# Token mixer of one decoder layer: the triangular inverse's recurrence spread over 128 partitions, its transpose made by products, the keys' chain given priority

## The chip, the cores and the metric

The kernel runs on one NeuronCore of a Trainium2 chip. The time is the device time of one execution in microseconds, on the slowest (here the only) core. The trace is that of one profiled execution of the program.

## The reference

One layer of an autoregressive decoder over 512 tokens of width 2048, all in float32. RMSNorm is followed by one input projection, whose columns feed three mixers in parallel: differential attention (4 heads), sliding-window attention (8 query heads, 2 key heads, window 128) and an RWKV-7 time mix (16 heads of 64). Their outputs are joined, projected, and added to the input; then come RMSNorm, a SwiGLU feed-forward of 5632 hidden units, a second addition, and a last RMSNorm. The change touches only the RWKV-7 part, whose definition is a scan over the tokens:

```python
kk = hs(k * k_k.astype(f32))
kk = kk / jnp.maximum(jnp.sqrt(jnp.sum(kk * kk, axis=-1, keepdims=True)), 1e-12)
k = k * (1.0 + (a - 1.0) * k_a.astype(f32))
...
y = wkv7_scan(r4, hs(decay), k4, v4, -kk, kk * a4)
...
def step(S, inp):
    r_t, w_t, k_t, v_t, a_t, b_t = inp
    sa = jnp.einsum('bhvk,bhk->bhv', S, a_t)
    S = S * w_t[:, :, None, :] + sa[..., None] * b_t[:, :, None, :] + v_t[..., None] * k_t[:, :, None, :]
    return S, jnp.einsum('bhvk,bhk->bhv', S, r_t)
```

## The kernel before, in words

**Dense work.** A projection item is 16 blocks of 128 input rows by 128 output columns against 512 tokens. Each float32 product is made of three products of a rounded format (high by high, high by low, low by high), so an item is 48 matmuls of 128 x 512, all through `mm`, line 130. `weights` (lines 203 to 208) loads half an item's weights by one DMA on the SP queue, casts the high part on ACT (line 207) and subtracts for the low part on DVE (line 208); the weights of the next item are asked for before the current one runs. The items run in this order: gates, then for each of eight pairs of RWKV heads k, r and v, then the attention heads, the output projection, and the feed-forward.

**Side work.** Everything of the mixers that is not a projection is written as Python generators in eight lanes. After each dense matmul `pump` lets every lane whose due time has come go one step. The due times come from `now`, a running estimate of the PE's time, and from `charge`, an estimate of when DVE and ACT will be done; `yield n` asks for n us of that estimate. The order of the PE's instructions is that order and is kept. On ACT, DVE, POOL and the DMA queues the compiler's scheduler puts the instructions in order by a priority, which is their place in the program unless a block raises it: `urgent` puts the state loop's copies at the program's start. When a projection is done, its `go` may have to wait for an older step (`need`): the k of a pair waits for the k of the pair before to be used up, the v for that pair's prep to end. Then only lanes run.

**A pair of RWKV heads.** Tokens are cut into 8 chunks of 64. For each pair:
- `rates` makes the decays; it begins when `prep` of the pair before has ended.
- `prep` normalises the keys (product `kn`, lines 509 to 512), makes `ar` (line 518, two buffers), `bk` (lines 526 and 531), turns `bk` on the PE in two halves (`bt`, line 540) into `bkn` once the state loop of the pair two before is done, makes the products `gr` (line 566) and masks them into `L`, `zl` and `gr` (line 574), and stores the four 32 x 32 diagonal blocks of each chunk of `L` to DRAM (`li`, line 585).
- `inverse` (lines 613 to 640) loads them as 32 matrices (2 heads, 2 blocks, 8 chunks), one whole matrix to a partition, and inverts the unit triangular matrices by a recurrence of 30 steps, two DVE instructions each (lines 629 and 630). It stores the result (`xi`) and, from a copy turned by ACT (line 633), its transpose (`xj`).
- `join` (lines 642 to 673) loads the inverted blocks back into `L` and the transposes of the first block of each head into `xn`, and makes the block off the diagonal by two sets of 16 products of 32 x 32 (`pt` and `po`).
- `chain` is the state loop over the 8 chunks, with products `z`, `u`, `S` and `y`; it begins when `post` of the pair before has read `y`. Its `y` products are the last readers of `ar`.
- `post` normalises and spills the result.

Of the kernel before, what the change touches and what calls it, by code (L numbers as in the profile page):

```python
# [8 lines left out]
F32 = mybir.dt.float32  # L9
F32R = mybir.dt.float32r  # L10
AF = mybir.ActivationFunctionType
ALU = mybir.AluOpType
AX = mybir.AxisListType

P = 128
# [4 lines left out]
C = 64  # L20
NCH = T // C
# [67 lines left out]
class Kernel:  # L89
    def __init__(self, tc, ins, out, dbg=None, stop=None):  # L90
        self.tc = tc
        self.nc = tc.nc
        self.i = ins
        self.out = out
        self.dbg = dbg or {}
        self.stop = stop
        self.lanes = [[], [], [], [], [], [], [], []]
        self.order = [self.lanes[j] for j in (2, 7, 6, 5, 0, 1, 3, 4)]
        self.done = set()
        self.flags = set()  # L100
        self.now = 0.0
        self.due = {}
        self.free = {"DVE": 0.0, "Activation": 0.0}
        self.last = 0.0
        self.slack = 0.3

    def col(self, name, j=0, n=P):
        c = COL[name] + j
        return self.cols[:n, c:c + 1]
# [383 lines left out]
    def prep(self, hp):  # L493
        nc, rp = self.nc, self.rp
        q = self.in_flight[hp]
        while "k" not in q or f"rates{hp}" not in self.done:
            yield
        W, V, a = q["W"], q["V"], q["a"]

        k = q["k"]  # L500
        rn = rp.tile([P, T], F32, tag="rn", name=f"rn{hp}")
        kk_g = self.col("k_k", hp)
        nc.scalar.activation(rn, k, AF.Square, scale=kk_g)
        yield
        ps = self.pm.tile([P, T], F32, tag="m", name=f"kn{hp}")
        self.mm(ps, self.cst("onesbd", P), rn, start=True, stop=True)
        kk = rp.tile([P, T], F32, tag="kk", name=f"kk{hp}")

        nc.scalar.activation(kk, ps, AF.Relu, bias=self.cst("knmin", 1))
        nc.scalar.activation(kk, kk, AF.Ln, bias=self.cst("kneps", 1))  # L510
        nc.scalar.activation(kk, kk, AF.Exp, scale=-0.5)
        nc.vector.scalar_tensor_tensor(out=kk, in0=k, scalar=kk_g, in1=kk, op0=ALU.mult, op1=ALU.mult)

        def c3(x):
            return x.rearrange("p (n c) -> p n c", c=C)

        ar = rp.tile([P, NCH, 2, C], F32, tag="ar", name=f"ar{hp}", bufs=2)
        nc.vector.scalar_tensor_tensor(out=ar[:, :, 0, :], in0=c3(kk), scalar=-1.0, in1=W[:, :, 0:64],
                                       op0=ALU.mult, op1=ALU.mult)
        bk = rp.tile([P, NCH, 2, C], F32, tag="bk", name=f"bk{hp}")  # L520
        nc.vector.tensor_tensor(out=kk, in0=kk, in1=a, op=ALU.mult)
        nc.scalar.activation(a, a, AF.Identity, bias=self.one_less("k_a", hp), scale=self.col("k_a", hp))

        for h in range(2):
            s = slice(h * 64, h * 64 + 64)
            nc.vector.tensor_tensor(out=bk[s, :, h, :], in0=c3(kk)[s], in1=V[s, :, 1:65], op=ALU.mult)
        nc.vector.tensor_tensor(out=a, in0=a, in1=k, op=ALU.mult)
        self.done.add(f"k{hp}")
        for h in range(2):
            s = slice(h * 64, h * 64 + 64)  # L530
            nc.vector.tensor_tensor(out=bk[s, :, 1 - h, :], in0=c3(a)[s], in1=V[s, :, 1:65], op=ALU.mult)
        yield

        while hp >= 2 and f"loop{hp - 2}" not in self.done:
# [2 lines left out]
        for u in range(2):  # L537
            ps = self.pm.tile([P, 4, P], F32, tag="m", name=f"bt{hp}_{u}")
# [15 lines left out]
        L = self.linv[hp % 2]  # L554
# [4 lines left out]
        for u in range(2):  # L559
            us = slice(4 * u, 4 * u + 4)  # L560
            yield
            ps = [self.pm.tile([P, 4, P], F32, tag="m", name=f"gr{hp}_{u}_{h}") for h in range(2)]
            for j in range(4):
                n = 4 * u + j
# [28 lines left out]
        ps = self.pm.tile([P, 4, P], F32, tag="m", name=f"vt{hp}")  # L593
# [3 lines left out]
        for h in range(2):  # L597
            for e in range(2):
                nc.scalar.copy(out=uvv[HALF[1 - h], :, e, h, :],
                               in_=ps[e * 64:e * 64 + 64, :, h * 64:h * 64 + 64])  # L600
# [4 lines left out]
        ps = self.pm.tile([P, T], F32, tag="m", name=f"bon{hp}")  # L605
# [7 lines left out]
    def inverse(self, q):  # L613

        nc, rp = self.nc, self.rp
        hp = q["hp"]
        yield 2.5


        x = rp.tile([32, 32, 32], F32, tag="i2", name="x")  # L620
        nc.sync.dma_start(out=x, in_=q["li"].rearrange("h b n s t -> (h b n) s t"))
        yield 2.5
        nc.vector.memset(x.rearrange("p s t -> p (s t)")[:, 0:1024:33], 1.0)
        tmp = rp.tile([32, 32, 32], F32, tag="i3", name="xt")
        for j in range(1, 31):
            n = 31 - j
            cl = x[:, j:j + 1, j + 1:32].to_broadcast([32, j, n])
            rw = x[:, 0:j, j:j + 1].to_broadcast([32, j, n])
            nc.vector.tensor_tensor(out=tmp[:, :j, :n], in0=cl, in1=rw, op=ALU.mult)
            nc.vector.tensor_tensor(out=x[:, 0:j, j + 1:32], in0=x[:, 0:j, j + 1:32], in1=tmp[:, :j, :n], op=ALU.add)  # L630
            yield max(self.free["DVE"] - self.now - 1.0, 0.1)
        xt = rp.tile([32, 32, 32], F32, tag="i1", name="xtt")
        nc.scalar.copy(out=xt[0:32].rearrange("p t s -> p s t"), in_=x)
        d = self.dp.tile([2, 2, NCH, 32, 32], F32, name=f"xi{hp}")
        dt = self.dp.tile([2, 2, NCH, 32, 32], F32, name=f"xj{hp}")
        nc.sync.dma_start(out=d.rearrange("h b n s t -> (h b n) s t"), in_=x)
        nc.sync.dma_start(out=dt.rearrange("h b n t s -> (h b n) t s"), in_=xt)
        q.update(xi=d, xj=dt)
        self.lanes[7].append((f"inv{hp}", self.join(q)))
        yield  # L640

    def join(self, q):

        nc, rp = self.nc, self.rp
        hp, L, blocks, d, dt = (q[n] for n in ("hp", "L", "blocks", "xi", "xj"))
        yield 4.5
        xn = rp.tile([P, NCH, 32], F32, tag="xn", name="xnn")
        for h, b, bl in blocks:
            nc.sync.dma_start(out=L[bl, :, bl], in_=d[h, b].rearrange("n s t -> s n t"))
            if not b:  # L650
                nc.sync.dma_start(out=xn[bl], in_=dt[h, b].rearrange("n t s -> t n s"))
        yield 3

        ps = self.pc.tile([P, NCH, 32], F32, tag="c", name="pt")
        for n in range(NCH):
            for h in range(2):
                lo, hi = blocks[2 * h][2], blocks[2 * h + 1][2]
                self.mm(ps[hi, n, :], L[lo, n, hi], xn[lo, n, :], start=True, stop=True)
        pt = rp.tile([P, NCH, 32], F32, tag="pt", name="pts")
        for h in range(2):  # L660
            hi = blocks[2 * h + 1][2]
            nc.scalar.copy(out=pt[hi], in_=ps[hi])
        yield
        ps = self.pc.tile([P, NCH, 32], F32, tag="c", name="po")
        for n in range(NCH):
            for h in range(2):
                lo, hi = blocks[2 * h][2], blocks[2 * h + 1][2]
                self.mm(ps[lo, n, :], pt[hi, n, :], L[hi, n, hi], start=True, stop=True)
        for h in range(2):
            lo, hi = blocks[2 * h][2], blocks[2 * h + 1][2]  # L670
            nc.scalar.copy(out=L[lo, :, hi], in_=ps[lo])
        yield
        self.lanes[2].append((f"loop{hp}", self.chain(q)))
# [603 lines left out]
```

## Time and profile before

| | us |
|---|---|
| median of three runs | 2480.77 (2480.57 to 2483.23) |
| the profiled execution | 2481.82 |
| its span, first to last instruction | 2480.0 |
| PE busy | 2419.3 |
| DVE busy | 1230.6 |
| ACT busy | 824.2 |
| POOL busy | 93.0 |

PE is the TensorE's matmuls, PEld its weight loads, DVE the VectorE, ACT the ScalarE, POOL the GpSimd, SP the engine that issues most of the DMAs. In rows that group instructions stand line, engine, operation, output and inputs by name, count, busy time, mean, and idle time before. In a timeline stand start and duration in us, then the instruction, and in brackets how long its engine had been idle and what ended that. PEclk is the share of its full clock that the TensorE was granted; it stood at 1.00 except in some stretches of 3.4 to 13.7 us. In a float32 product each matmul leaves two records in the trace, so 16 products show as 32. The RWKV pairs fill the span from about 50 to 660 us, attention goes on to about 890, and from there on the trace is dense work almost alone.

### The profile page before, as it was taken

What the parts mean: (1) busy time and instruction counts of PE and PEld (TensorE: products, weight loads), DVE (VectorE), ACT (ScalarE), POOL (GpSimd) and SP (SyncE); (2) the same over time, 40 slices, a digit from 0 to 9 for tenths busy, and PEclk for the clock granted to TensorE, in tenths of its full rate; (3) what the DMA queues carried; (4) which work ended last, traced back from release to release, by engine and by line L of the source; (5) the groups of instructions that cost most, each with busy time, mean ns of one, the idle gap of its engine ahead of it and who ended that gap; (6) DMA issues with size and microseconds to landing.
All of it is one profiled execution on the core that took longest, in us unless ns stands there. A gap on an engine that the chain in (4) does not pass through costs nothing.

```text
span 2480.0 us, 30228 instructions
## 1 busy us (share of the span) xinstructions
PE 2419.3 (98%) x12072; PEld 1921.0 (77%) x12072; DVE 1230.6 (50%) x2113; ACT 824.2 (33%) x1383; POOL 93.0 (4%) x117
## 2 busy tenths in 40 slices
PE   8999999989999999999999999999999999999997
PEld 6776666667677778888888888888888888888887
DVE  7587777776454544434343434343434334343437
ACT  5454555544443433322222222222222222222224
POOL 3000000000000002100000000000000000000006
PEclk9999999999999999999999999999999999999999
DMA  5222221213222423322322223232232322322224
GB/s 175 88 80 72 69 81 49 79 60 96 84 83 79 162 94 128 99 96 95 101 94 101 95 95 101 94 99 97 94 101 94 99 97 94 101 94 99 97 94 136
DMA packets 99054, 238.43 MB, mean 96 GB/s; under 512 B 30426, under 2 KB 39266, under 8 KB 98914
## 3 DMA queue, kind: packets, MB, share of 16 engines
q1 hardware_dynamic: 94018, 229.81, 28.7%
q10 hardware_dynamic: 4896, 6.69, 0.8%
q8 instruction: 95, 1.56, 0.2%
q14 instruction: 45, 0.37, 0.0%
HBM read 224.93 MB, written 11.53 MB: 95 GB/s over the span
## 4 chain that ended last, share of the span: by engine, by line
PE 91%; DVE 6%; ACT 1%; issue 1%; DMA 1%; POOL 0%; SPq 0%; DVEq 0%; ACTq 0%; POOLq 0%
PE pg L130 19%; PE pu L130 19%; PE pd L130 19%; PE po L130 7%; PE pd_k L130 4%; PE pd_r L130 3%; PE pd_v L130 2%; PE pd_va L130 2%; PE pd_qb L130 2%; PE pd_qa L130 2%; PE pd_ka L130 1%; PE z L130 1%; PE pd_l L130 1%; PE y L130 1%; PE gr L130 1%
## 5 line engine op out<-in xcount | busy, mean ns | idle before, releaser
L130 PE MATMUL pd<-al,wh_wd 128*128 128x512 f32 (+1 forms) x768 | 285.3, 371 | 0.5 <-DVE al L1127 0.5
L130 PE MATMUL pd<-ah,wh_wd 128*128 128x512 f32 (+1 forms) x768 | 285.5, 372 | 0.4 <-DVE y L1146 0.4
L130 PE MATMUL pd<-ah,wl_wd 128*128 128x512 f32 (+1 forms) x768 | 285.2, 371 | 0.0
L130 PE MATMUL pu<-x1h,wh_wu 128*128 128x512 f32 x704 | 274.3, 390 | 0.0
L130 PE MATMUL pu<-x1h,wl_wu 128*128 128x512 f32 x704 | 273.9, 389 | 0.0
L130 PE MATMUL pu<-x1l,wh_wu 128*128 128x512 f32 x704 | 273.9, 389 | 0.0
L130 PE MATMUL pg<-x1h,wh_wg 128*128 128x512 f32 x704 | 273.9, 389 | 0.0
L130 PE MATMUL pg<-x1h,wl_wg 128*128 128x512 f32 x704 | 273.9, 389 | 0.0
L130 PE MATMUL pg<-x1l,wh_wg 128*128 128x512 f32 x704 | 273.9, 389 | 0.0
L1146 DVE TENSOR_TENSOR y<-y,pd 128x512 f32<-128x512 f32 (+1 forms) x192 | 122.7, 642 | 207.7 <-PE pd L130 207.6
L207 ACT CAST wh_wd<-raw_wd 128x1024 fp32r<-128x1024 f32 x96 | 100.9, 1052 | 356.9 <-PE pd L130 177.2
L207 ACT CAST wh_wu<-raw_wu 128x1024 fp32r<-128x1024 f32 x88 | 92.7, 1053 | 366.7 <-PE pu L130 144.5
L207 ACT CAST wh_wg<-raw_wg 128x1024 fp32r<-128x1024 f32 x88 | 92.7, 1054 | 362.8 <-PE pg L130 144.9
L208 DVE TENSOR_TENSOR wl_wg<-raw_wg,wh_wg 128x1024 fp32r<-128x1024 f32 x88 | 107.8, 1225 | 171.4 <-ACT wh_wg L207 171.4
L208 DVE TENSOR_TENSOR wl_wu<-raw_wu,wh_wu 128x1024 fp32r<-128x1024 f32 x88 | 107.8, 1225 | 133.4 <-ACT wh_wu L207 133.4
L130 PEld LDWEIGHTS pd<-al,wh_wd 128*128 128x128 f32 x768 | 144.7, 188 | 25.7 <-DVE al L1127 0.8
L130 PEld LDWEIGHTS pd<-ah,wh_wd 128*128 128x128 f32 x768 | 144.7, 188 | 25.5 <-issue 0.5
L130 PEld LDWEIGHTS pd<-ah,wl_wd 128*128 128x128 f32 x768 | 144.7, 188 | 25.0
L130 PEld LDWEIGHTS pu<-x1h,wh_wu 128*128 128x128 f32 x704 | 132.2, 188 | 27.6 <-issue 0.2
L130 PEld LDWEIGHTS pu<-x1l,wh_wu 128*128 128x128 f32 x704 | 132.2, 188 | 27.6 <-issue 0.2
L130 PEld LDWEIGHTS pg<-x1l,wh_wg 128*128 128x128 f32 x704 | 132.2, 188 | 27.4
L130 PEld LDWEIGHTS pg<-x1h,wh_wg 128*128 128x128 f32 x704 | 132.2, 188 | 27.4
(340 smaller groups left out, 4155.1 us busy)
## 6 DMA issues: line engine op xcount, KB each, us to landing
raw_wd<-in_w_down SPq DMA_DIRECT2D x96, 512.0 KB, 3.2
raw_wg<-in_w_gate SPq DMA_DIRECT2D x88, 512.0 KB, 3.7
raw_wu<-in_w_up SPq DMA_DIRECT2D x88, 512.0 KB, 3.7
raw_wo<-in_w_out SPq DMA_DIRECT2D x32, 512.0 KB, 3.3
raw_k<-in_w_in SPq DMA_DIRECT2D x16, 512.0 KB, 3.7
raw_r<-in_w_in SPq DMA_DIRECT2D x16, 512.0 KB, 3.9
raw_v<-in_w_in SPq DMA_DIRECT2D x16, 512.0 KB, 3.8
x<-in_xT SPq DMA_DIRECT2D x16, 256.0 KB, 4.6
```

What stands on the lines that cost most here:

```text
L130: self.tc.keep_in_program_order(self.nc.tensor.matmul(out, lhsT, rhs, start=start, stop=stop))
L207: nc.scalar.copy(out=hi[:, :kn * m], in_=s)
L208: nc.vector.tensor_tensor(out=lo[:, :kn * m], in0=s, in1=hi[:, :kn * m].bitcast(F32), op=ALU.subtract)
L1146: nc.vector.tensor_tensor(out=o, in0=o, in1=ps, op=ALU.add)
```

## The change

Three things in one diff.
- The recurrence: each of the 32 matrices is loaded four times, into the partitions 32 g to 32 g + 31 for g from 0 to 3, and partition group g makes the rows g, g + 4, g + 8 and so on, kept in a tile `y` of 8 rows by 32. `y` begins as the unit matrix, by memsets on POOL. A step multiplies row j of the loaded matrix with column j of the rows that lie at or above it, so that there are j // 4 + 1 of them. It has 31 steps. Four DMAs store `y`, in pieces of one row.
- The transpose: no turned copy, no second store and no loads of it. Once the inverted blocks have been loaded into `L`, 16 products with a 32 x 32 identity put the transposes in PSUM (`px`), and two copies on ACT bring them to `xn`.
- The keys' chain: from the first activation on `kn` to the last write of `bk`, ACT's and DVE's instructions stand in a block that lowers their place in the order of priority by 300 instructions.

```diff
+        self.lead = 300
...
+        with self.tc.high_priority(self.lead):
+
+            nc.scalar.activation(kk, ps, AF.Relu, bias=self.cst("knmin", 1))
...
-        x = rp.tile([32, 32, 32], F32, tag="i2", name="x")
-        nc.sync.dma_start(out=x, in_=q["li"].rearrange("h b n s t -> (h b n) s t"))
-        yield 2.5
-        nc.vector.memset(x.rearrange("p s t -> p (s t)")[:, 0:1024:33], 1.0)
-        tmp = rp.tile([32, 32, 32], F32, tag="i3", name="xt")
-        for j in range(1, 31):
-            n = 31 - j
-            cl = x[:, j:j + 1, j + 1:32].to_broadcast([32, j, n])
-            rw = x[:, 0:j, j:j + 1].to_broadcast([32, j, n])
-            nc.vector.tensor_tensor(out=tmp[:, :j, :n], in0=cl, in1=rw, op=ALU.mult)
-            nc.vector.tensor_tensor(out=x[:, 0:j, j + 1:32], in0=x[:, 0:j, j + 1:32], in1=tmp[:, :j, :n], op=ALU.add)
+        x = rp.tile([P, 32, 32], F32, tag="i2", name="x")
+        y = rp.tile([P, 8, 32], F32, tag="i1", name="xy")
+        yf = y.rearrange("p i t -> p (i t)")
+        nc.gpsimd.memset(yf, 0.0)
+        for g in range(4):
+            gs = slice(32 * g, 32 * g + 32)
+            nc.sync.dma_start(out=x[gs], in_=q["li"].rearrange("h b n s t -> (h b n) s t"))
+            nc.gpsimd.memset(yf[gs, g:256:36], 1.0)
+        yield 3.5
+        tmp = rp.tile([P, 8, 32], F32, tag="i3", name="xt")
+        for j in range(31):
+            n, m = 31 - j, j // 4 + 1
+            cl = x[:, j:j + 1, j + 1:32].to_broadcast([P, m, n])
+            rw = y[:, 0:m, j:j + 1].to_broadcast([P, m, n])
+            nc.vector.tensor_tensor(out=tmp[:, :m, :n], in0=cl, in1=rw, op=ALU.mult)
+            nc.vector.tensor_tensor(out=y[:, 0:m, j + 1:32], in0=y[:, 0:m, j + 1:32], in1=tmp[:, :m, :n], op=ALU.add)
             yield max(self.free["DVE"] - self.now - 1.0, 0.1)
-        xt = rp.tile([32, 32, 32], F32, tag="i1", name="xtt")
-        nc.scalar.copy(out=xt[0:32].rearrange("p t s -> p s t"), in_=x)
-        d = self.dp.tile([2, 2, NCH, 32, 32], F32, name=f"xi{hp}")
-        dt = self.dp.tile([2, 2, NCH, 32, 32], F32, name=f"xj{hp}")
-        nc.sync.dma_start(out=d.rearrange("h b n s t -> (h b n) s t"), in_=x)
-        nc.sync.dma_start(out=dt.rearrange("h b n t s -> (h b n) t s"), in_=xt)
+        d = self.dp.tile([2, 2, NCH, 8, 4, 32], F32, name=f"xi{hp}")
+        for g in range(4):
+            nc.sync.dma_start(out=d[:, :, :, :, g].rearrange("h b n i t -> (h b n) i t"), in_=y[32 * g:32 * g + 32])
...
         yield 4.5
+        for h, b, bl in blocks:
+            nc.sync.dma_start(out=L[bl, :, bl], in_=d[h, b].rearrange("n i g t -> (i g) n t"))
+        yield 3.5
+
+        ps = self.pc.tile([P, NCH, 32], F32, tag="c", name="px")
+        for n in range(NCH):
+            for h in range(2):
+                lo = blocks[2 * h][2]
+                self.mm(ps[lo, n, :], L[lo, n, lo], self.cst("ident", P)[lo, lo], start=True, stop=True)
         xn = rp.tile([P, NCH, 32], F32, tag="xn", name="xnn")
-        for h, b, bl in blocks:
-            nc.sync.dma_start(out=L[bl, :, bl], in_=d[h, b].rearrange("n s t -> s n t"))
-            if not b:
-                nc.sync.dma_start(out=xn[bl], in_=dt[h, b].rearrange("n t s -> t n s"))
-        yield 3
+        for h in range(2):
+            lo = blocks[2 * h][2]
+            nc.scalar.copy(out=xn[lo], in_=ps[lo])
+        yield
```

More of the change, by code (lines that the diff above doesn't have):

```diff
@@ L507, in prep @@
         kk = rp.tile([P, T], F32, tag="kk", name=f"kk{hp}")
[L509 to L531, printed above, removed]
+        with self.tc.high_priority(self.lead):
+            nc.scalar.activation(kk, ps, AF.Relu, bias=self.cst("knmin", 1))
+            nc.scalar.activation(kk, kk, AF.Ln, bias=self.cst("kneps", 1))
+            nc.scalar.activation(kk, kk, AF.Exp, scale=-0.5)
+            nc.vector.scalar_tensor_tensor(out=kk, in0=k, scalar=kk_g, in1=kk, op0=ALU.mult, op1=ALU.mult)
+            def c3(x):
+                return x.rearrange("p (n c) -> p n c", c=C)
+            ar = rp.tile([P, NCH, 2, C], F32, tag="ar", name=f"ar{hp}", bufs=2)
+            nc.vector.scalar_tensor_tensor(out=ar[:, :, 0, :], in0=c3(kk), scalar=-1.0, in1=W[:, :, 0:64],
+                                           op0=ALU.mult, op1=ALU.mult)
+            bk = rp.tile([P, NCH, 2, C], F32, tag="bk", name=f"bk{hp}")
+            nc.vector.tensor_tensor(out=kk, in0=kk, in1=a, op=ALU.mult)
+            nc.scalar.activation(a, a, AF.Identity, bias=self.one_less("k_a", hp), scale=self.col("k_a", hp))
+            for h in range(2):
+                s = slice(h * 64, h * 64 + 64)
+                nc.vector.tensor_tensor(out=bk[s, :, h, :], in0=c3(kk)[s], in1=V[s, :, 1:65], op=ALU.mult)
+            nc.vector.tensor_tensor(out=a, in0=a, in1=k, op=ALU.mult)
+            self.done.add(f"k{hp}")
+            for h in range(2):
+                s = slice(h * 64, h * 64 + 64)
+                nc.vector.tensor_tensor(out=bk[s, :, 1 - h, :], in0=c3(a)[s], in1=V[s, :, 1:65], op=ALU.mult)
@@ L632, in inverse @@
-        xt = rp.tile([32, 32, 32], F32, tag="i1", name="xtt")
-        nc.scalar.copy(out=xt[0:32].rearrange("p t s -> p s t"), in_=x)
-        d = self.dp.tile([2, 2, NCH, 32, 32], F32, name=f"xi{hp}")
-        dt = self.dp.tile([2, 2, NCH, 32, 32], F32, name=f"xj{hp}")
-        nc.sync.dma_start(out=d.rearrange("h b n s t -> (h b n) s t"), in_=x)
-        nc.sync.dma_start(out=dt.rearrange("h b n t s -> (h b n) t s"), in_=xt)
-        q.update(xi=d, xj=dt)
+        x = rp.tile([P, 32, 32], F32, tag="i2", name="x")
@@ L639, in inverse @@
+        d = self.dp.tile([2, 2, NCH, 8, 4, 32], F32, name=f"xi{hp}")
+        for g in range(4):
+            nc.sync.dma_start(out=d[:, :, :, :, g].rearrange("h b n i t -> (h b n) i t"), in_=y[32 * g:32 * g + 32])
+        q.update(xi=d)
         self.lanes[7].append((f"inv{hp}", self.join(q)))
@@ L644, in join @@
         nc, rp = self.nc, self.rp
-        hp, L, blocks, d, dt = (q[n] for n in ("hp", "L", "blocks", "xi", "xj"))
+        hp, L, blocks, d = (q[n] for n in ("hp", "L", "blocks", "xi"))
         yield 4.5
-        xn = rp.tile([P, NCH, 32], F32, tag="xn", name="xnn")
-        for h, b, bl in blocks:
-            nc.sync.dma_start(out=L[bl, :, bl], in_=d[h, b].rearrange("n s t -> s n t"))
-            if not b:
-                nc.sync.dma_start(out=xn[bl], in_=dt[h, b].rearrange("n t s -> t n s"))
-        yield 3
+        for h, b, bl in blocks:
[3 more added lines that the diff above has]
+        for n in range(NCH):
+            for h in range(2):
+                lo = blocks[2 * h][2]
+                self.mm(ps[lo, n, :], L[lo, n, lo], self.cst("ident", P)[lo, lo], start=True, stop=True)
+        xn = rp.tile([P, NCH, 32], F32, tag="xn", name="xnn")
+        for h in range(2):
+            lo = blocks[2 * h][2]
+            nc.scalar.copy(out=xn[lo], in_=ps[lo])
+        yield
         ps = self.pc.tile([P, NCH, 32], F32, tag="c", name="pt")
```

## The prediction

> **What bounds the kernel now.** I read the busy times first, then who waits for whom on the PE, then the granted clock around those waits, and last the timeline of one pair of heads.
>
> ```profile
> PE 2419.3 (98%) x12072; PEld 1921.0 (77%) x12072; DVE 1230.6 (50%) x2113; ACT 824.2 (33%) x1383; POOL 93.0 (4%) x117
> ```
> The PE is busy 98% of the span and carries the chain that ended last, so no edit on DVE or ACT is worth anything by its own duration. It pays only where it shortens a wait of the PE, and its price is what it adds to the PE's stream. The wait of the PE that this change goes for, with its total, number and longest:
>
> ```profile
> PE bt L134 <- DVE bk L531: 19.6, 8, 3.6
> ```
> One wait per pair: the transposes of `bk` (line 540) reach the PE before the keys' chain has written `bk`. A wait also costs clock. Of the stretches that follow five of those waits the first, then the sum of the five, then the two longest slow ones (engines' busy time, number of instructions, PEclk):
>
> ```profile
> 94.15:97.56 3.41, 3.41 (x13) 2.72 (x12) 0.14 (x1) 0.59 (x1) 0.00 (x0) 0.50 0.11 41
> ```
> ```profile
> sum 17.07, PE 15.86 PEld 12.41 DVE 10.15 ACT 5.08 POOL 0.29; mean PE 3.17 PEld 2.48 DVE 2.03 ACT 1.02 POOL 0.06
> ```
> ```profile
> 370.63:384.28 13.65, 12.51 (x65) 9.25 (x65) 4.80 (x13) 5.06 (x17) 0.00 (x0) 0.50 0.13 33
> 503.75:513.99 10.24, 9.86 (x49) 7.08 (x50) 4.30 (x12) 4.81 (x15) 0.00 (x0) 0.50 0.12 27
> ```
> At a clock of 0.50 half of the PE's busy time is lost: about 15.86 / 2 = 7.9 us in the five short stretches and (12.51 + 9.86) / 2 = 11.2 us in the two long ones. What trips it shows in four stretches of 3.4 us ahead of a decision:
>
> ```profile
> 278.46:281.88 3.42, 1.72 (x10) 0.81 (x8) 3.36 (x7) 2.75 (x5) 0.00 (x0) 1.00 0.02 7
> 356.95:360.37 3.42, 1.96 (x11) 1.00 (x9) 3.38 (x8) 2.87 (x6) 0.00 (x0) 1.00 0.41 141
> 408.15:411.56 3.41, 2.33 (x14) 1.33 (x12) 3.37 (x7) 3.09 (x7) 0.00 (x0) 1.00 0.16 62
> 555.00:558.36 3.36, 1.83 (x17) 1.56 (x18) 3.13 (x11) 0.00 (x0) 0.00 (x0) 1.00 0.48 156
> ```
> The first and last (PE busy 1.72 and 1.83) were followed by half clock, the middle two (1.96 and 2.33) were not. In these rows the edge lies between 1.83 and 1.96 us of work in 3.4 us.
> The Trainium skill, page "TensorE: Matmul & The Clock Gate", section "HAM oscillation — how this bites in real kernels", puts it as "no PE-idle gaps >~3.4µs". By that rule only the longest of the eight waits could trip the clock, and the clock term below would be about 1.6 us instead of 6.3, the sum -13.5. The rows above disagree: a wait of 2.2 us was enough where it fell into one stretch.
>
> **The keys' chain put first (prep, lines 509 to 531).** Pair 3, the DVE's timeline and then the PE's:
>
> ```profile
> 276.79 0.69 DVE L518 SCALAR_TENSOR_TENSOR ar<-kk,W 128x512 f32<-128x512 f32 x1 [0.42 <-PE y L130]
> 277.40 0.39 DVE L629 TENSOR_TENSOR xt<-x 32x240 f32<-32x240 f32 x1
> 277.72 0.67 DVE L521 TENSOR_TENSOR kk<-kk,a 128x512 f32<-128x512 f32 x1
> 278.32 0.39 DVE L630 TENSOR_TENSOR x<-x,xt 32x240 f32<-32x240 f32 x1
> 278.64 1.37 DVE L526 TENSOR_TENSOR bk<-kk,IW 64x512 f32<-64x512 f32 x2
> 280.04 0.69 DVE L527 TENSOR_TENSOR a<-a,k 128x512 f32<-128x512 f32 x1
> 280.65 0.39 DVE L629 TENSOR_TENSOR xt<-x 32x238 f32<-32x238 f32 x1
> 280.97 1.37 DVE L531 TENSOR_TENSOR bk<-a,IW 64x512 f32<-64x512 f32 x2
> ```
> ```profile
> 279.79 0.39 PE L130 MATMUL pd_r<-xl,wh_r 128*128 128x512 f32 x1
> 282.40 0.90 PE L134 MATMUL bt<-cc,bk 128*128 128x128 f32 x3 [2.22 <-DVE bk L531]
> ```
> Two things hold `bk` up. Three instructions of the recurrence stand between those of the chain; and line 518 had to wait for a `y` matmul, because `ar` has two buffers and the state loop of the pair two before was still reading one of them. Priority takes away the first and not the second. Without the three, the chain takes 0.69 + 0.67 + 1.37 + 0.69 + 1.37 = 4.8 us, some 4.7 with the small overlap of starts, and ends at 276.79 + 4.7 = 281.5. The PE was free at 279.79 + 0.39 = 280.2. So **1.3 us of the 2.2 stays** wherever `ar` is the gate. A wait of 1.3 leaves about 2.1 us of work in a stretch of 3.4, just above the edge found above, so I take the clock to stay up in four of the five places.
>
> Pairs 0 and 1 have no earlier reader of `ar`. Pair 1, ACT:
>
> ```profile
> 133.31 0.69 ACT L509 ACTIVATE kk<-kn,cc 128x512 f32<-128x512 f32 x1 [3.06 <-PE kn L130]
> 134.03 0.72 ACT L510 ACTIVATE kk<-kk,cc 128x512 f32<-128x512 f32 x1
> 134.66 1.03 ACT L207 CAST wh_k<-raw_k 128x1024 fp32r<-128x1024 f32 x1
> 135.60 0.63 ACT L511 ACTIVATE kk<-kk 128x512 f32<-128x512 f32 x1
> ```
> ```profile
> 136.37 1.21 DVE L208 TENSOR_TENSOR wl_k<-raw_k,wh_k 128x1024 fp32r<-128x1024 f32 x1
> 137.51 0.74 DVE L512 SCALAR_TENSOR_TENSOR kk<-k,cols,kk 128x512 f32<-128x512 f32 x1
> ```
> ```profile
> 140.19 0.39 PE L130 MATMUL pd_k<-xh,wl_k 128*128 128x512 f32 x1
> ```
> ```profile
> 144.91 0.75 PE L134 MATMUL bt<-cc,bk 128*128 128x128 f32 x4 [2.52 <-DVE bk L531]
> ```
> From 133.31 to 144.9 the chain took 11.6 us. Its own work is 0.69 + 0.72 + 0.63 + 0.74 + 4.8 = 7.6, so up to 4.0 us can go, more than the wait of 2.5: here the wait vanishes. For pair 0 I take the mean of the eight, 19.6 / 8 = 2.45. Together -5.0 us. The other six hold 19.6 - 5.0 = 14.6 us, of which 6 x 1.3 = 7.8 stays: -6.8 us. The clock: 4/5 of 7.9, -6.3 us.
>
> This is paid by what is moved past. With a lead of 300 instructions the chain stands ahead of the recurrence, the shifts and the weights' casts (lines 207, 208), not ahead of the state loop's copies, whose priority is the program's start. In pair 1 `wl_k` ended at 137.6 and was used at 140.19, a margin of 2.6 us. Put behind the chain, whose ACT part then ends at 135.4 and whose DVE part runs 0.74 + 4.8 = 5.5 us to 140.9 or a little before, it would end near 141.6: +1.4 us there. In the other pairs I take nothing. If that cover is absent, it is the slower rival below.
>
> **The recurrence over 128 partitions (inverse, lines 620 to 637).** The whole recurrence of pair 4, and everything on the engines in its time:
>
> ```profile
> 388.50:431.30 42.80, 19.02 (x60) 1.00 0.18 59
> ```
> ```profile
> 388.50:431.30 42.80, 40.57 (x232) 28.85 (x232) 38.94 (x100) 20.86 (x45) 0.31 (x3) 1.00 0.18 59
> ```
> ```profile
> L629 DVE TENSOR_TENSOR xt<-x x240: 141/336/399, 122.1 to 597.8; 32x30 f32<-32x30 f32 x8, 32x84 f32<-32x84 f32 x8, 32x130 f32<-32x130 f32 x8, 32x168 f32<-32x168 f32 x8
> ```
> Sixty instructions take 19.0 us of DVE. Afterwards there are 62, of (j // 4 + 1) x (31 - j) elements per partition instead of j x (31 - j): at most 76 instead of 240, 50 on average. Between 141 ns at 30 elements and 399 at 240 lies 1.2 ns an element, so a mean of about 170 to 210 ns (the more partitions do not lengthen it; all rows of 128 partitions above run at the same rate per element) and 10.5 to 13 us in all; I take 12.5. The DVE was busy 38.94 of 42.80 us, 19.9 of it with other work. If that other work keeps its share of about 0.47, the recurrence ends after 12.5 / 0.53 = 24 to 27 us instead of 43: **16 us earlier**. Also gone are the turned copy on ACT, behind which its store stood, and two loads of its result:
>
> ```profile
> 431.31 2.04 ACT L633 COPY xtt<-x 32x1024 f32<-32x1024 f32 x1 [0.51 <-DVE x L630]
> ```
> Added in the same chain: three more loads of `x` and three more stores of `xi`, each at the 0.47 us that SP takes to issue one of these,
>
> ```profile
> 437.18 0.94 SPq L649 DMA_DIRECT2D linv<-xi  x2
> ```
> so 1.4 us each set, and the new product, its two copies and a turn of the planner, taken as the step from `pt` to `po`:
>
> ```profile
> 445.54 0.69 PE L130 MATMUL pt<-xnn,linv 32*32 32x32 f32 x32
> ```
> ```profile
> 449.33 0.69 PE L130 MATMUL po<-linv,pts 32*32 32x32 f32 x32
> ```
> That is 3.8 us, so the inverse is ready some 16 - 3 - 3.8 + 2 = 11 us sooner. No engine gains by that directly. It moves the state loop of a pair ahead, and with it the release of `ar` and of `bkn` for the pair after next. Where it is late today the projections themselves are held (`v` of one pair waits for prep of the pair before), and the PE is left with small dependent products: that is the two stretches of 13.65 and 10.24 us at half clock. In the same products it waits for the masks of line 574 to free PSUM:
>
> ```profile
> PE gr L130 <- DVE gr L574: 5.7, 6, 2.4
> ```
> The price of both is 11.2 + 5.7 = 16.9 us. Eleven us may cover it wholly or hardly; nothing here runs in a shorter order, so the bounds are 0 and 16.9, and I take half: -8.5 us.
>
> The stores of `xi` go in pieces of 128 B now, before in 4 KB:
>
> ```profile
> li<-linv SPq DMA_DIRECT2D x32, 32.0 KB, 1.6
> ```
> ```profile
> xi<-x SPq DMA_DIRECT2D x8, 128.0 KB, 1.9
> ```
> `li` is written in such pieces already and lands in 1.6 us, so a quarter of `xi` is taken at that, hidden by the 4.5 us that `join` waits. Per pair the SP queue issues 16 transfers instead of 13; weight loads stand behind them, and these are prefetched an item ahead. Exposed, it would be 3 x 0.47 x 8 = 11 us. The five memsets go to POOL, 4% busy, and end before the loads of `x` land.
> The Trainium skill, page "DMA: Bandwidth & Descriptors", section "Specifications", asks for 512 B and more, since below that the DMA engine reads, changes and writes back. It speaks against these stores; by it the sum would be the same as long as the 4.5 us hide them, and the landing of `li` gives no sign of such a loss.
>
> **The product with the identity (join).** Sixteen products of 32 x 32 a pair, as many and of the same shape as those of `pt`:
>
> ```profile
> 367.05 0.96 PE L130 MATMUL pt<-xnn,linv 32*32 32x32 f32 x32
> 367.93 0.72 PE L130 MATMUL gr<-ar,bk 64*128 64x128 f32 x8
> ```
> From one start to the next 0.88 us; 8 pairs make **+7.0 us**, all on the bounding engine. PE waits there only if the loads of `L` land later than the planner's 3.5 us; the same gap of 3 us shows no such wait for `pt` today, so nothing is added, with up to 1 us a pair as the other bound.
>
> **Sum.** -5.0 - 6.8 - 6.3 - 8.5 + 7.0 + 1.4 = -18.2 us. The profiled execution took 2481.82 us (span 2480.0), 1.05 above the median of the runs, 2480.77: 2463.6 for it, **2462.5 for the median**. By the bounds of its terms this case reaches from 2449 to 2474.
>
> **Rivals.**
> *Everything comes free.* If the state loop ends before the keys' chain of the pair after next starts, `ar` is no gate, all eight waits go, and with them all slow stretches: -19.6 - 7.9 - 16.9 + 7.0 = -37 us, 2443. For it: the DVE, 91% busy during a recurrence, loses a third of that work. Against it: the loop would have to gain all that it is late by in six pairs.
> *It does not do what it says.* The order on DVE is decided by when `ar` is released, and the planner lets the recurrence go no faster than its other lanes. Pairs 0 and 1 gain 5.0, the others 2, the clock 2, against 7.0 and 1.4: -0.6 us, 2480.
> *Slower: the weights come late.* Place: lines 207 and 208. Each chain holds the DVE 5.5 us against a margin of 2.6, so a cast that becomes ready at its start makes the PE wait 2.9 us and trips the clock for another 1.7: 4.6 us a hit. From three hits of eight on it decides: 13.8 + 7.0 - 11.8 = +9; with five, 23 + 7.0 - 11.8 = +18, 2499. For it: pair 1 shows such a cast in the middle of the chain. Against it: a pair has only six casts, and most chains start with `ar`, at no fixed distance to them.
>
> **Chances.** Forecast 0.54, everything free 0.17, no effect 0.18, slower 0.11. I count a difference as seen from 0.2%, 5 us, which is about what the three runs shown can tell. Of the no-effect case about a quarter falls below that line: faster 0.54 + 0.17 + 0.04 = 0.75, same 0.14, slower 0.11. The range of 2440 to 2481 leaves out the slower case, a part of the no-effect case and the very end of the free one, 2 in 10.
>
> **What would show it.** Right: the `bt` wait at about 8 us in total, near nothing in pairs 0 and 1; line 518 still released by a `y` matmul; the recurrence in 24 to 27 us with some 12.5 of DVE; fewer stretches at 0.50, the two long ones shorter; eight new groups of 32 records at about 0.9 us. Wrong: waits of the PE for `wl` (line 208), a wait for the loads of `L` in front of the new product, or slow stretches as long as before with the `bt` wait gone, which would say that the clock follows something else.

## The result, and the profile after

The changed kernel takes **2498.35 us** (median of four runs, 2493.15 to 2500.34) against 2480.77: 17.6 us slower, ratio 1.0065 with a 95% interval of 1.0048 to 1.0083. The forecast was 2462.5 with a range of 2440 to 2481. The profiled execution took 2499.81 us with a span of 2498.0, 18.0 above that of before. From line 106 on line numbers stand one higher than before (`mm` is line 131, the casts 208 and 209), from 509 on two and more (`ar` 520, `bk` 528 and 533); the recurrence is lines 636 and 637, the products with the identity go through `mm`.

The page's first part, after:

```profile
PE 2426.2 (97%) x12328; PEld 1922.1 (77%) x12328; DVE 1186.6 (48%) x2121; ACT 815.9 (33%) x1391; POOL 98.6 (4%) x157
```
The PE is busy 6.9 us more than before (2419.3) and idle 2498.0 - 2426.2 = 71.8 us in place of 60.7. So of the 18.0 us the PE worked 6.9 and stood still 11.1. DVE lost 44 us of work, which bought nothing by itself.

Where it happened, by busy time of the engines in two stretches of the span (length, PE, PEld, DVE, ACT, POOL, PEclk, DMA share, GB/s), before:

```profile
60.00:760.00 700.00, 665.84 (x4078) 479.10 (x4077) 473.86 (x1110) 339.45 (x728) 3.04 (x30) 0.97 0.26 77
760.00:2400.00 1640.00, 1636.97 (x7328) 1343.59 (x7327) 662.80 (x871) 418.69 (x548) 26.72 (x15) 1.00 0.30 100
```
and after:

```profile
60.00:760.00 700.00, 655.01 (x4255) 466.39 (x4254) 420.18 (x1095) 324.92 (x725) 8.21 (x65) 0.96 0.26 77
760.00:2400.00 1640.00, 1636.40 (x7326) 1341.91 (x7325) 663.87 (x885) 419.11 (x554) 26.73 (x15) 1.00 0.31 100
```
The later stretch is the same in both. In the first one, that of the RWKV pairs, the PE is idle 700 - 655.0 = 45.0 us in place of 34.2: +10.8. What filled it are the waits of the PE, after (total, number, longest):

```profile
PE bt L135 <- DVE bk L533: 19.9, 8, 3.3
PE px L131 <- DMA linv<-xi: 16.1, 4, 7.6
```
The wait that the change went for is as long as before, 19.9 against 19.6. A new one of 16.1 us has come: the new product `px` reaches the PE before the inverted blocks have been loaded into `L`, in three of the eight pairs (twice in pair 0, once in pairs 6 and 7). The wait of `gr` for the masks, 5.7 us before, is gone. 0.3 + 16.1 - 5.7 = 10.7, close to the 10.8 of idle time; the other waits moved by less than 2 us each, some up and some down.

The clock is not in the difference. All stretches at 0.50 between 60 and 760 us taken together (the sum over them), before:

```profile
sum 44.37, PE 41.63 PEld 31.37 DVE 22.47 ACT 14.95 POOL 0.29; mean PE 5.20 PEld 3.92 DVE 2.81 ACT 1.87 POOL 0.04
```
after, with the longest one ahead of the sum:

```profile
161.07:174.72 13.65, 9.54 (x108) 7.42 (x110) 0.92 (x3) 2.92 (x8) 0.73 (x5) 0.50 0.29 63
...
sum 51.18, PE 41.97 PEld 31.23 DVE 11.33 ACT 12.94 POOL 1.46; mean PE 4.66 PEld 3.47 DVE 1.26 ACT 1.44 POOL 0.16
```
Half of the PE's work in them is lost: 41.63 / 2 = 20.8 us before, 41.97 / 2 = 21.0 after. The two long stretches at 370 and 504 us are gone, and this one of 13.65 us, around the first wait of `px`, and one of 6.8 us at 608, around the last, have come instead; two more of 6.8 us stand at waits for `bk`, at 472 and 537 us.

The products themselves, by the groups of instructions (count, busy time, mean ns, idle time ahead and what ended it):

```profile
L131 PE MATMUL px<-cc,linv 32*32 32x32 f32 x256 | 7.1, 204 | 16.3 <-DMA linv<-xi 16.1
```
7.1 + 10.8 + 0.2 = 18.1, against the 18.0 of the spans. With that the account is closed, and the question is why `px` waits.

Pair 0, the PE; then the other two pairs that waited, 6 and 7; then SP's queue in pair 0:

```profile
158.44 0.40 PE L131 MATMUL pd_r<-xl,wh_r 128*128 128x512 f32 x1
164.65 0.28 PE L131 MATMUL px<-cc,linv 32*32 32x32 f32 x2 [5.81 <-DMA linv<-xi]
165.46 1.06 PE L131 MATMUL px<-cc,linv 32*32 32x32 f32 x30 [0.54 <-DMA linv<-xi]
166.45 0.80 PE L131 MATMUL pd_r<-xh,wl_r 128*128 128x512 f32 x1
```
```profile
554.69 1.03 PE L131 MATMUL px<-cc,linv 32*32 32x32 f32 x32 [2.16 <-DMA linv<-xi]
610.80 1.38 PE L131 MATMUL px<-cc,linv 32*32 32x32 f32 x32 [7.62 <-DMA linv<-xi]
```
```profile
158.31 2.64 SPq L641 DMA_DIRECT2D xi<-xy  x4
161.00 1.58 SPq L587 DMA_DIRECT2D li<-linv  x3
162.76 1.79 SPq L652 DMA_DIRECT2D linv<-xi  x4
```
The four stores of `xi` could be issued from 158.31 on, right behind the recurrence; the loads of `L` follow at 162.76, behind three stores of another pair, and the product starts for good at 165.46. The PE had reached it at 158.84. So the PE's order, which is fixed when the program is built, has `px` less than a microsecond behind the recurrence's end, and the data need seven. DVE in the same pair shows that the recurrence itself is late:

```profile
120.37 0.68 DVE L611 TENSOR_TENSOR bv<-bon,v 128x512 f32<-128x512 f32 x1
122.72 1.24 DVE L481 TENSOR_TENSOR_SCAN cum<-keep,sg 128x520 f32<-128x520 f32 x1 [1.67 <-ACT sg L377]
124.00 0.70 DVE L484 TENSOR_TENSOR sg<-cum 128x520 f32<-128x520 f32 x1
125.99 0.17 DVE L490 TENSOR_TENSOR D<-W,IW 128x7 f32<-128x7 f32 x1 [1.29 <-ACT IW L488]
126.16 0.19 DVE L636 TENSOR_TENSOR xt<-x,xy 128x31 f32<-128x31 f32 x1
127.07 0.69 DVE L361 TENSOR_TENSOR h_r<-pd_r,rstd_a 128x512 f32<-128x512 f32 x1 [0.72 <-PE pd_r L131]
127.68 0.18 DVE L637 TENSOR_TENSOR xy<-xy,xt 128x31 f32<-128x31 f32 x1
```
No step of the recurrence waits for its loads, here or in another pair. The first one stands in DVE's queue behind the scan, line 484 and `D`, which wait for ACT, and the second behind `h_r`, which waits for the PE. The loads of `x` were issued from 117.91 to 119.6 and are listed with 3.6 us to landing, which puts the last at about 123 (an estimate from these two numbers). This was my theory for the experiments: **the recurrence stands late in DVE's queue, so `L` lands after the point at which the PE's fixed order asks for it.** The rivals: the way behind the recurrence (stores, loads) alone makes the wait; the products themselves are the cost; the priority block is.

### The profile page after: what moved, and what is told of

Same layout as the page of the kernel before. It is cut to its first block, busy times and chain, and to the rows that moved or that the text cites. A ratio compares the mean times of both kernels' runs of the same rounds, so it can differ in the third digit from the quotient of the medians.

```text
span 2498.0 us, 30841 instructions
## 1 busy us (share of the span) xinstructions
PE 2426.2 (97%) x12328; PEld 1922.1 (77%) x12328; DVE 1186.6 (48%) x2121; ACT 815.9 (33%) x1391; POOL 98.6 (4%) x157
## 4 chain that ended last, share of the span: by engine, by line
PE 88%; DVE 2%; ACT 1%; DMA 1%; issue 1%; POOL 0%; SPq 0%; DVEq 0%; ACTq 0%; POOLq 0%
PE pg L131 19%; PE pu L131 19%; PE pd L131 18%; PE po L131 7%; PE pd_r L131 3%; PE pd_v L131 3%; PE pd_k L131 2%; PE pd_va L131 2%; PE pd_ka L131 2%; PE pd_qb L131 2%; PE pd_qa L131 2%; PE z L131 1%; PE y L131 1%; PE S L131 1%; PE gr L131 1%; PE g L131 1%
## 5 line engine op out<-in xcount | busy, mean ns | idle before, releaser
L131 PEld LDWEIGHTS pu<-x1h,wl_wu 128*128 128x128 f32 x704 | 132.1, 188 | 27.5
L131 PEld LDWEIGHTS pg<-x1h,wl_wg 128*128 128x128 f32 x704 | 132.1, 188 | 27.5
```

The costliest lines, as they stand in the source:

```text
L131: self.tc.keep_in_program_order(self.nc.tensor.matmul(out, lhsT, rhs, start=start, stop=stop))
```

## The experiments

A table first. Idle is 700 us less the PE's busy time between 60 and 760 us; lost is half of the PE's busy time in the stretches at 0.50; the sum is the change of both against before, with 7.1 us where the products with the identity are in (their busy time in the change; it is 5.6 to 7.1 in the runs that have them). It gives the span of eleven of these within 3 us and of the other two (e4, e8) within 4.5, so these three terms are where the time goes. All columns but the median are of one profiled execution, and those of e8 and e10 were 4.3 and 3.5 us shorter than their medians.

| kernel | median, us | idle, us | lost, us | products, us | sum, us | span against before, us |
|---|---|---|---|---|---|---|
| before | 2480.8 | 34.2 | 20.8 | | | |
| after | 2498.4 | 45.0 | 21.0 | 7.1 | +18.1 | +18.0 |
| e1_no_lead | 2494.1 | 44.2 | 17.7 | 7.1 | +14.0 | +12.9 |
| e2_lead_only | 2480.0 | 34.9 | 21.3 | | +1.3 | -0.1 |
| e3_join_late | 2489.0 | 38.8 | 17.5 | 7.1 | +8.4 | +7.2 |
| e4_px_only | 2487.0 | 33.1 | 26.3 | 7.1 | +11.5 | +7.0 |
| e5_one_load | 2524.9 | 54.0 | 37.2 | 7.1 | +43.3 | +45.4 |
| e6_dve_turn | 2499.0 | 51.2 | 20.6 | | +16.8 | +17.6 |
| e7_load_and_turn | 2517.6 | 63.2 | 23.5 | | +31.7 | +34.3 |
| e8_turn_late | 2479.6 | 33.8 | 18.3 | | -2.9 | -6.5 |
| e9_two_queues | 2475.9 | 33.4 | 8.5 | 7.1 | -5.9 | -5.9 |
| e10_all | 2482.3 | 37.4 | 15.3 | | -2.3 | -3.0 |
| e11_queues_no_lead | 2483.4 | 35.3 | 15.4 | 7.1 | +2.8 | +1.8 |
| e12_queues_turn | 2474.2 | 34.4 | 15.0 | | -5.6 | -7.2 |

**One part at a time.** The priority taken out of the change, and the priority alone:

```diff
-        with self.tc.high_priority(self.lead):
+        with contextlib.nullcontext():
```


> The changed kernel without the raised priority of the keys' chain; recurrence and identity products stay. Theory A (the new product reaches the PE before the loads of L have landed, because the planner counts the short recurrence as done earlier than DVE finishes it): the wait of px for linv stays near 16 us in total and the time stays at 2493 to 2500. Rival B (the raised priority pushes the recurrence and the casts back and so makes the loads late): the px wait falls below 5 us and the time to 2484 or less.

> The kernel before with nothing but the raised priority of the keys' chain. Theory A: a block whose instructions wait for each other gets nothing from priority, since something else that is ready goes between them; bt wait 17 to 21 us as before, time 2476 to 2486. Rival B: 2488 or more. The prediction's step: bt wait about 8 us, 2465 to 2470.

Without the priority the change takes 2494.06 (ratio to before 1.005, 1.0033 to 1.0067); the priority alone 2480.01 (0.9999, 0.999 to 1.0009). Alone it does nothing, and its wait for `bk` is that of before, 19.6:

```profile
PE bt L135 <- DVE bk L533: 19.7, 8, 3.7
```
One of these waits in the changed kernel shows why the chain isn't shorter. Pair 4 on DVE, then the PE:

```profile
337.62 0.69 DVE L520 SCALAR_TENSOR_TENSOR ar<-kk,W 128x512 f32<-128x512 f32 x1 [1.14 <-PE y L131]
338.23 1.22 DVE L209 TENSOR_TENSOR wl_r<-raw_r,wh_r 128x1024 fp32r<-128x1024 f32 x1
339.37 0.68 DVE L523 TENSOR_TENSOR kk<-kk,a 128x512 f32<-128x512 f32 x1
339.97 0.68 DVE L549 TENSOR_TENSOR ar<-r,W 128x512 f32<-128x512 f32 x1
340.57 1.38 DVE L528 TENSOR_TENSOR bk<-kk,IW 64x512 f32<-64x512 f32 x2
341.98 0.69 DVE L529 TENSOR_TENSOR a<-a,k 128x512 f32<-128x512 f32 x1
342.71 1.39 DVE L533 TENSOR_TENSOR bk<-a,IW 64x512 f32<-64x512 f32 x2
```
```profile
344.15 0.66 PE L135 MATMUL bt<-cc,bk 128*128 128x128 f32 x4 [3.14 <-DVE bk L533]
```
A cast and line 549 still stand between the chain's steps, 1.9 us of a wait of 3.14, in a block that has priority over both; what is left without them is 1.2. And the chain still begins when a `y` matmul releases `ar`. My reading, which no run tested, is that a step that needs the one before is not ready while that one runs, so that the gap goes to whatever is, whatever its priority.

The products alone, with the recurrence of before:

```diff
-        xt = rp.tile([32, 32, 32], F32, tag="i1", name="xtt")
-        nc.scalar.copy(out=xt[0:32].rearrange("p t s -> p s t"), in_=x)
...
+        ps = self.pc.tile([P, NCH, 32], F32, tag="c", name="px")
...
+                self.mm(ps[lo, n, :], L[lo, n, lo], self.cst("ident", P)[lo, lo], start=True, stop=True)
```


> The kernel before, recurrence on 32 partitions as it was, no raised priority, but with the transpose by identity products instead of the turned copy, its store and its loads. Theory A: with the long recurrence the planner's estimate fits DVE, px waits at most 3 us in total, the added products cost 7 us: 2482 to 2490. Rival D (the identity product itself is what waits, whatever the recurrence): px wait over 10 us and 2492 or more.

2486.97 against 2480.51, 1.0024 (1.0014 to 1.0033): +6.5 us, and no wait of `px`. The products are a third of the loss, and they need not wait: with the recurrence of before they don't.

**The place of the product in the PE's order.** The planner's delay between the loads of `L` and `px`:

```diff
-        yield 3.5
+        yield 9.5
```


> The changed kernel with one number changed: the planner's pause between the loads of L and the identity product is 9.5 instead of 3.5 of its us. Theory A: the px wait goes below 2 us, the slow stretches at pairs 0 and 7 go too, and the time falls by the 16 us of wait and some 8 us of clock, less a few us for later state loops: 2473 to 2482. Rival C (the loss is the added products and the changed order of the PE, the px wait only stands where another wait would stand): 2492 or more although the px wait is gone.

2488.96, 1.0028 (1.0018 to 1.0038). The wait of `px` falls from 16.1 to 5.4 us, and 9.4 of the 17.6 us are back. The same product, asked for later, costs less. The expectation, a wait under 2 us and at most 2482, was missed: 5.4 us of waiting and the products are still in.

**The place of the recurrence in DVE's queue.** First I made the four loads of `x` one DMA:

```diff
-            nc.sync.dma_start(out=x[gs], in_=q["li"].rearrange("h b n s t -> (h b n) s t"))
+        nc.sync.dma_start(out=x, in_=q["li"].rearrange("h b n s t -> (h b n) s t").partition_broadcast(4))
```


> The changed kernel with the four loads of the system x made one (the same 64 KB, one DMA whose source is read four times). If the products with the identity wait because the recurrence starts late on VectorE (its first step 4 to 7 us after the four loads have landed, behind the scan, IW and D that stand before it in the queue), then its first step now stands directly behind bv, the products' wait for the loads of L falls from 16.1 us in all to below 5 us, and the time to 2482 to 2489 us (2498 less some 11 to 16). If the wait is set by the way behind the recurrence alone (store, three stores of the identity, two loads: 8 us), it stays at 12 us or more and the time at 2493 us or above.

(The expectation's 64 KB is wrong: it is 512 KB, 128 KB read four times.) 2524.93, 1.0171 (1.0146 to 1.0195): far slower, and neither theory had it. DVE, pair 0:

```profile
121.23 0.68 DVE L611 TENSOR_TENSOR bv<-bon,v 128x512 f32<-128x512 f32 x1
129.68 0.19 DVE L636 TENSOR_TENSOR xt<-x,xy 128x31 f32<-128x31 f32 x1 [7.76 <-DMA x<-li]
129.90 0.19 DVE L637 TENSOR_TENSOR xy<-xy,xt 128x31 f32<-128x31 f32 x1
```
The first step now stands directly behind `bv`, as I wanted. But the DMA, issued at 118.72, is not there until 129.68, and for 7.76 us DVE stands with everything that is queued behind that step: 38.2 us in the eight pairs, listed under the instructions that touch `x`:

```profile
  DMA x<-li: 38.2, 8
```
So the run left the theory open, though the wait of `px` did fall to 1.6 us; what it shows is the price of the opposite error, a step queued ahead of its data.

Then two of the four loads went to GpSimd's queue, with all else as in the change:

```diff
-            nc.sync.dma_start(out=x[gs], in_=q["li"].rearrange("h b n s t -> (h b n) s t"))
+            (nc.gpsimd if g % 2 else nc.sync).dma_start(out=x[gs], in_=q["li"].rearrange("h b n s t -> (h b n) s t"))
```


> The changed kernel with two of the four loads of x issued from GpSimd's queue in place of SyncE's; TensorE's order stays as it is and on VectorE the first steps of the recurrence come to stand ahead of D, h_r, the cast of v's weights and others that they stood behind. If the products' wait for L comes of the recurrence standing late in VectorE's queue, it ends 2 to 5 us earlier in each pair, and the wait falls from 16.1 to 2 to 8 us: 2484 to 2492 us. If the way behind the recurrence (the stores, then the loads) makes the wait, it stays at 13 us or more and the time at 2495 us or above.

**2475.91, 0.9986 (0.9977 to 0.9995)**: 22.4 us below the change and 4.6 below the kernel before. The PE's instructions stand in the same order as in the change; DVE's do not (and in a few places ACT's). Pair 0:

```profile
122.14 1.24 DVE L481 TENSOR_TENSOR_SCAN cum<-keep,sg 128x520 f32<-128x520 f32 x1 [1.67 <-ACT sg L377]
123.42 0.70 DVE L484 TENSOR_TENSOR sg<-cum 128x520 f32<-128x520 f32 x1
124.03 0.18 DVE L636 TENSOR_TENSOR xt<-x,xy 128x31 f32<-128x31 f32 x1
124.25 0.19 DVE L637 TENSOR_TENSOR xy<-xy,xt 128x31 f32<-128x31 f32 x1
124.48 0.19 DVE L636 TENSOR_TENSOR xt<-x,xy 128x30 f32<-128x30 f32 x1
```
The loads did not land sooner to speak of: they are listed at 3.4 us to landing from SP's queue and 4.2 from GpSimd's, against 3.6 in the change. The first step moved ahead of `D`, the second ahead of `h_r`. The recurrence of pair 0 ran from 124.0 to 151.3 instead of 126.2 to 158.2, while the PE reached `px` at 157.9 instead of 158.8. That of pair 7 ended 7.3 us before the PE was at `px`, instead of 3.3. The wait:

```profile
PE px L131 <- DMA linv<-xi: 1.9, 1, 1.9
```
and the sum of the stretches at 0.50:

```profile
sum 17.07, PE 17.07 PEld 12.27 DVE 6.44 ACT 3.41 POOL 0.10; mean PE 3.41 PEld 2.45 DVE 1.29 ACT 0.68 POOL 0.02
```
The time lies 8 us under the range given for it, because the lost clock went with the wait, 12.5 us beside 11.6 us of idle time, and I had counted the wait alone. The order of DVE's queue is written when the program is built. It changes when only the queue of two loads does; I read this as an order made from an assumed time of arrival, which with four loads on one queue lies after the real one, and with one load (above) before it.

The same edit on two other bases, the change without the priority (2494.06) and the change with `L` turned on DVE (2498.96, below):

> The kernel with two queues for x (2475.9), without the priority block. If that kernel's time comes of the recurrence starting earlier on VectorE, this one has it too: wait of the products under 5 us, 2472 to 2480 us. If it was the place of the priority block's instructions among the recurrence's that made it, this one falls back: 2484 us or above.

> The kernel with two queues for x (2475.9), with the other orientation of L by two transposes on VectorE in place of the products (delay 3.5 and priority as in the changed kernel). If the products' 6.5 us on TensorE can be had back once L arrives in time: 2466 to 2471 us. If TensorE then only comes sooner to a wait for L or for bk, and to more stretches at the half clock, as with the delay 6.5 and no priority (2482.3): 2476 to 2484 us.

2483.42 (1.0008, 0.9999 to 1.0016) and **2474.18 (0.9966, 0.9953 to 0.9979)**. So two queues are worth 22.4, 10.6 and 24.8 us on the three bases, and the wait in front of the first product that reads `L` falls from 16.1 to 1.9, from 13.0 to 3.7 and from 22.9 to 5.3 us. e11 had the wait of its first case but a time between the two cases, 7.5 us above e9: idle time differs by 1.9 us, lost clock by 6.9. e12 lies between its cases too: it does without the products and is only 1.7 us faster than e9, since it lost 6.5 us more of clock. With the priority the change was 4.3 us slower than without it, here 7.5 faster: a shift of the pattern, not a gain of the chain.

**The products off the PE.** The other orientation of `L` by two 32 x 32 block transposes on DVE:

```diff
-                self.mm(ps[lo, n, :], L[lo, n, lo], self.cst("ident", P)[lo, lo], start=True, stop=True)
...
-            nc.scalar.copy(out=xn[lo], in_=ps[lo])
+            nc.vector.transpose(out=xn[lo], in_=L[lo, :, lo])
```


> The changed kernel with the other orientation of L made on VectorE, by two transposes of 32x32 blocks, in place of the 64 products with the identity on TensorE and their copies. The products cost +7.0 us by my sum (and +6.5 by the run that had them alone), and their wait was 16.1 us. If the wait belongs to the arrival of L, it moves to the next product that reads L (pt) and stays at 12 us or more: 2488 to 2492 us. If the wait came from the products' own place in the order, it goes too: 2474 to 2480 us.

> Both edits: one load of x, and the other orientation on VectorE. If the late start on VectorE and the products on TensorE are the two costs, this is the short recurrence without either: 2472 to 2482 us, at or under the kernel before. If the short recurrence is worth what my sum gave it (some 18 us with the stretches at the half clock), 2462 to 2470 us. If the wait for L is not of the late start, 2486 us or above.

2498.96 (1.0069, 1.0053 to 1.0086), 7 us above the range given for it: 7.1 us of the PE's work taken away and not a microsecond gained. The wait went to `pt` and grew by the same 7 us:

```profile
PE pt L131 <- DVE xnn L658: 22.9, 9, 6.9
```
That is what a wait for data does that come at their own time: whatever is saved in front of it is spent waiting. e7, 2517.55 (1.0152, 1.0137 to 1.0168), has DVE blocked by the one load again.

**What the short recurrence is worth.** Without priority and without products, with the delay 9.5; and with two queues and the delay 6.5:

> The changed kernel without the priority block, the other orientation of L made by two transposes on VectorE, and the planner's delay between the loads of L and the first product that reads it 9.5 in place of 3.5. What is left of the change is the short recurrence alone, with neither the 64 products nor (by the run with 9.5 alone, 5.4 us of 16.1 left) most of the wait for L. If a shorter recurrence is worth what my sum gave it: 2462 to 2470 us. If the recurrence was hidden behind TensorE's dense work before and its length is worth nothing: 2478 to 2484 us, since the run with 9.5 gave 2489.0 and the products cost 6.5. If the products' wait simply moves to pt as in the run with the transposes: 2488 us or above.

> The two edits together (transposes on VectorE, two queues for x), without the priority block, and the delay 6.5. If late start and products are all that the change costs, nothing of the wait for L is left, and the time lies at the kernel before or a little under: 2472 to 2482 us. If the length of the recurrence counts: 2462 to 2470 us. If other work on VectorE is pushed back by the recurrence that now starts earlier (casts of weights, chains of the next pair): 2486 us or above with new waits for VectorE in front of TensorE.

2479.59 (0.9997, 0.9988 to 1.0006) and 2482.26 (1.0005, 0.9996 to 1.0014). e8 holds the new recurrence without the products and with 2.2 us of waiting for `L`, and it is the kernel before to within 0.1%. The shorter recurrence did reach the PE there: `pt` came 5 to 18 us earlier than before in the eight pairs, in a profiled execution that was 6.5 us shorter in all. But what the earlier loop should have removed is still there: 4.4 us of the wait of `gr` for the masks, 5.7 before, and a stretch of 10.24 us at half clock from 489.5 us. Shortening it gained nothing there. e10 missed its first case by 0.3 us, with 2.8 us of waiting left in front of `pt`; e12, which differs from it by the priority and the delay, is 8 us faster. The kernels with little wait for `L` (before, e8 to e12) lie between 2474 and 2484, and I can't take that spread apart further than the table does.

## Why the prediction was wrong

The forecast was -18.2 us and the span grew by 18.0. Term by term, forecast and then measured: the waits for `bk` -11.8 and +0.3; the clock -6.3, with a share of the -8.5 besides, and +0.2; the waits of `gr`, in the -8.5, and -5.7; the products +7.0 and +7.1; the weights +1.4 and no such wait; the wait of `px` 0 and +16.1. So two steps failed, of about the same size: a wait put at nothing, and a gain that did not come.

**The first step that failed** is the one on the new product: "PE waits there only if the loads of `L` land later than the planner's 3.5 us; the same gap of 3 us shows no such wait for `pt` today, so nothing is added, with up to 1 us a pair as the other bound." It was 16.1 us in three pairs, the longest 7.6. The delay of 3.5 us isn't the whole distance: before, `pt` came 7 to 18 us after the recurrence's end in the eight pairs (14 in pair 4, 431.30 to 445.54), and that hid the stores, the queue and the loads. In the changed kernel the data are there 7 to 11 us after the recurrence's end in the three pairs that waited, and the PE is at `px` 0.6 us after it in pair 0, 3.3 in pair 7 and 7.7 in pair 6: the product was moved up, and the recurrence was not by as much, because with four loads on one queue it stands behind other work on DVE. e3 (product later) and e9 (recurrence sooner, the PE's order untouched) each take most of the wait away.

**The second is the keys' chain**, -5.0 and -6.8 and -6.3 of clock: nothing came. The wait for `bk` is 19.9 against 19.6 and the clock loses 21.0 against 20.8; e2, the priority alone, shows the same. In pairs 0 and 1, where the wait was to vanish, it is 2.0 and 1.5 us, against 2.0 and 2.5 before. The reading of `ar` as the gate held in part (DVE stood idle for `y` ahead of line 520 in three pairs of eight). What failed is that priority takes other instructions out of the chain. With the 1.9 us between the steps of pair 4 taken off, 1.2 of the wait would be left, the 1.3 of the working; but they are still there, and other ones than before.

**The recurrence itself** was sized well: 12.5 us of DVE in 24 to 27 us were predicted. After, DVE's time for it in the window of pair 4's recurrence:

```profile
379.20:412.50 33.30, 13.10 (x62) 0.95 0.20 64
```
13.1 us in 33; between 23 and 33 in the eight pairs. The elapsed time was under-estimated, since the rest of DVE's queue stood in between.

**Its worth**, -8.5 between 0 and 16.9: the wait of `gr` did go, 5.7 us, and so did the two long stretches at half clock. But the two stretches around waits of `px` lost 6.9 us, and those at the waits for `bk` 12.4 in place of 7.9, so the clock came out even. In e8, with little of these waits, the total is 0.0 within 0.1%, though the loop's data came 5 to 18 us earlier, about the 11 us of the working. So the step from an earlier state loop to fewer waits and slow stretches did not hold, and the lower bound of 0 was the right end there. e9 and e12 lie 4.6 and 6.3 us under the kernel before; how much of that is the recurrence and how much the clock, no run separates.

**The products**, +7.0: 7.1 by the groups of instructions, +6.5 by e4. Right. **The weights**, +1.4 and the slower rival of 2499: its time was hit by chance, its mechanism not; no wait of the PE for the low parts of the weights stands in the list of after. Of the signs named ahead, "a wait for the loads of `L` in front of the new product" is the one that came. The bounds of 2449 and 2474 don't follow from the terms as given: with 0 to 16.9 for the recurrence's worth and 0 to 8 for the wait of `px`, the sum goes from 2454 to 2479. The measured 2498.35 lies outside either.

## What to carry to other kernels

When a chain is shortened whose result another engine takes at a fixed place in its order, ask what slack that place had, and which work in it (stores, a shared queue, loads) does not get shorter; here the wait appeared exactly there. The order of a queue is fixed when the program is built, as I read it from an assumed arrival of the data: an instruction placed too late stands behind others, one placed too early stops everything behind it, and which queue issues the loads was enough to change the time by 11 to 25 us. Work taken off the bounding engine ahead of a wait for data isn't gained (e6); with most of the wait gone 1.7 us were (e12 against e9), while the clock took 6.5 more.

## What the runs showed of the hardware

**One load of 512 KB was slower than four of 128 KB.** From its issue at 118.72 to the first use at 129.68 it took 11.0 us; the four are listed at 3.6 us each. DMA share and GB/s (last two columns), e5 and then after, in stretches in which they ran:

```profile
126.00:128.00 2.00, 2.00 (x11) 1.65 (x10) 0.00 (x0) 0.00 (x0) 0.00 (x0) 1.00 0.33 98
128.00:130.00 2.00, 2.00 (x10) 1.66 (x9) 0.29 (x2) 0.00 (x0) 0.00 (x0) 1.00 0.23 85
```
```profile
118.00:120.00 2.00, 2.00 (x8) 1.23 (x7) 0.78 (x1) 1.19 (x2) 0.00 (x0) 1.00 0.61 154
```
A mean busy share of 0.23 to 0.33 is the work of about four to five of the 16 DMA engines, that of other transfers included. The Trainium skill, page "DMA: Bandwidth & Descriptors", section "Rules for kernel authors", says that an outermost dimension of fewer than 16, as a repeated source has, keeps the whole DMA on at most as many engines. The outermost dimension here is the four repeats, and the shares in the trace are in line with it.

**The same wait cost clock in one run and not in another.** Pair 0's wait for `bk` is 1.98 us in e9 and 1.99 in e11. The stretches of 3.4 us, on the grid of each run's stretches at 0.50, in which it lies and the one after, e9 and then e11:

```profile
91.65:95.07 3.42, 1.49 (x9) 1.32 (x10) 2.52 (x4) 0.59 (x1) 0.00 (x0) 1.00 0.50 153
95.07:98.48 3.41, 3.41 (x19) 2.82 (x18) 1.27 (x2) 2.26 (x3) 0.00 (x0) 1.00 0.02 5
```
```profile
89.28:92.69 3.41, 1.47 (x7) 0.89 (x5) 3.32 (x5) 0.81 (x2) 0.00 (x0) 1.00 0.27 77
92.69:96.10 3.41, 3.37 (x10) 2.79 (x11) 0.69 (x1) 0.58 (x1) 0.00 (x0) 0.50 0.23 82
```
The PE was busy 1.49 and 1.47 us of the stretch, by the prediction's edge of 1.83 to 1.96 both should trip, and one did. In e9 the idle time lies in the first part of the stretch, in e11 in the last. So busy time in a stretch of this grid isn't what decides, or not alone; what does stays open. A stretch costs 1.7 us (half of 3.41). With waits for `bk` of 22.1 and 22.8 us in all, e9 lost 8.5 us of clock and e11 15.4. Executions of one and the same kernel differ in this way too: of the eleven of e8 the shortest, 2473.46, had a mean granted clock of 0.991 and the longest, 2483.20, 0.986. So differences of a few us between kernels of one design can be of this kind.
